# Chunk states of two groups in one two-bank tile, u copied on VectorE, kernel products issued by kind, in a two-layer attention and S5 kernel

## The chip, the cores and the metric

One core of one Trainium2 chip runs the whole network in one launch. The metric is the device time in microseconds (us) of one execution; smaller is better. TensorE is called PE here, VectorE DVE, ScalarE ACT, GpSimd POOL, and SyncE, which only issues DMAs here, SP.

## The reference

Two layers work on 2,048 latent tokens and 256 context tokens of width 1,024. Layer 0 is windowed attention. Layer 1, where the change lies, is a bidirectional diagonal state-space layer (S5): 64 groups of 16 channels, each with 64 complex states and two directions.

```python
for dirn in range(2):
    a_bar = exp(lam * dt)
    b_bar = ((a_bar - 1.0) / lam)[..., None] * b_mat
    bu = einsum('gph,blgh->blgp', b_bar, ug)
    xs = diag_scan(a_bar, bu with the context's last state added at 0)
    y = y + einsum('ghp,blgp->blgh', c_mat, xs).real
out = s5_output(y, z, w_glu, w_out)   # gelu, GLU, silu(z) gate, projection
```

## The kernel before

The state-space layer is done in chunks of 16 tokens: 144 chunks, 16 of them context. It runs in phases, each a Python method. PE does the matmuls of all of them.

**Phase 4** (`phase4`) makes the chunk states `sall`, laid out as 128 partitions x 144 chunks x (re, im) x 64 groups. It goes over 8 slabs of 8 groups. For a slab it needs two tables `er`, `ei` per half slab (4 groups); in even slabs they come by DMA from `ed` (L1416), in odd slabs DVE and POOL build them (L1422 to L1427: two POOL products `em`, four DVE operations). For each group PE transposes the tables into `ep` (four transposes, L1439), ACT copies `ep` to SBUF as `esb` (L1441); PE transposes the group's `u` into `up` (two, L1446), and DVE, or for one group in four (`UPA`, L51) ACT, copies it back over `uy` (L1450, L1448). Then `chunk_states` (L1376) makes four matmuls of 144 columns into the PSUM tile `st` (L1380; the trace has eight records, since a float32 matmul is recorded twice) and ACT writes them to `sall` in three instructions: one direction as it stands (L1382), the other reversed in two pieces (L1383, L1384). Each writes single float32 elements, because neighbouring elements of `sall` in a partition are different groups. `chunk_states` runs one group behind (`LAG4`). `PB` (L50) gives the buffers of `ep`, `up` and `st` in PSUM. Once per slab `up` also carries the context's `u` (L1399, L1400).

The **scan** over chunks on DVE and the **z projection** on PE (`zproj`) follow and run side by side.

**Phase 5** (`phase5`) makes the layer's output in 16 quarters `q` of 4 groups. In steady state `out(q, plan)` goes through the tokens of `P5P` (L36): `S0 S1` state matmuls (L1724) from `xT`, which ACT gathers out of `sall` (L1717, L1719); `K` the kernel products of q+1 (`ker`, L1681 on); `G` tables of q+2 (`gen`); `N` their preparation (`prep`); `O0 O1` own-chunk matmuls (L1735); `B2 B3` both kinds for two more groups; `T` transposes of finished output (L1749). After `O` and `B`, ACT applies Gelu (`ysl`, L1792). `gen` has ACT copy two small parts of the table tile `tab` into `gr` and `gi` (L1582), `prep` has it copy two parts into `cb` (L1671) and four into `g4` (L1676). `ker` accumulates in one PSUM tile `kps`: eight products of 64 columns (L1688), four of 16 columns from `cb` (L1693), each right behind one of the first four, and one with the identity (L1687) ahead of the last. ACT copies `kps` to `ks` (L1697), SP stores `ks` to DRAM as `qqd` (L1699) and loads it back, skewed, as the matrices `mq` (L1708) that `O` and `B` use.

A scheduler sets the order on each engine from the program and its own simulated times; instructions given to `keep` stay in program order. Each engine then runs its list in order.

## Time and profile before

| | us |
|---|---|
| three runs | 2605.39, 2609.28 (median), 2610.87 |
| the profiled execution | 2605.47 |
| its span in the trace | 2603.7 |
| phase 4, first to last transpose or state matmul | about 1527 to 1661 |
| z projection | about 1661 to 1858 |
| phase 5 | about 1859 to 2057 |

The span is the time from the first to the last instruction of the profiled execution; 1.8 us lie around it. "Busy" is the time in which an engine has an instruction running; PE's matmuls overlap, so a busy PE need not be at its peak. A stage is read by its own rows: the share of a whole run says little about which engine holds it up.

### The profile page before, as it was taken

How to read it: one execution, taken by the hardware profiler on the slowest of the kernel's cores; microseconds unless marked ns; L12 is line 12 of the kernel's file. 1: busy time of each engine (PE TensorE's matmuls, PEld its weight loads, DVE VectorE, ACT ScalarE, POOL GpSimd, SP SyncE). 2: the span in 40 equal slices, each digit the busy share in tenths (PEclk: the TensorE clock that was granted, in tenths of full speed). 3: DMA queues.
4: the chain of work that ended last, by engine and by line, in shares of the span. 5: the costliest groups of instructions: out<-in, count | busy, mean ns of one | idle time of the engine just before them, and what ended most of it. 6: DMA issues, size and time to landing. Idle time of an engine off the chain costs nothing. (4 is left out here: it accounts for less than half of the span.)

```text
span 2603.7 us, 43687 instructions
## 1 busy us (share of the span) xinstructions
PE 2493.4 (96%) x15838; PEld 2251.8 (86%) x15838; DVE 1555.8 (60%) x3866; ACT 1151.3 (44%) x2651; POOL 817.2 (31%) x701
## 2 busy tenths in 40 slices
PE   7999999998999999999999999899999899999998
PEld 5999989997988999999899988799877688888887
DVE  4773276636898888888732865698576421012454
ACT  3301210136777777777644349611399610001221
POOL 0321331213545455555432222101265222121221
PEclk9999999998999999999999999999999999999999
DMA  8555456477454434434275552376444322223542
GB/s 282 174 166 169 146 168 195 142 192 196 101 139 106 102 91 104 111 93 104 89 202 176 211 158 83 107 237 236 148 100 103 85 81 81 65 81 122 170 140 79
DMA packets 402312, 360.23 MB, mean 138 GB/s; under 512 B 82921, under 2 KB 345129, under 8 KB 402097
## 3 DMA queue, kind: packets, MB, share of 16 engines
q1 hardware_dynamic: 296216, 286.03, 38.3%
q10 hardware_dynamic: 105880, 71.41, 8.6%
q8 instruction: 126, 2.06, 0.3%
q14 instruction: 90, 0.73, 0.1%
HBM read 250.83 MB, written 106.51 MB: 137 GB/s over the span
## 5 line engine op out<-in xcount | busy, mean ns | idle before, releaser
L117 PE MATMUL mm<-hhl,whi 128*128 128x384 f32 x848 | 285.0, 339 | 1.6 <-DVE whi L109 1.6
L118 PE MATMUL mm<-hhl,whi 128*128 128x384 f32 x848 | 285.3, 337 | 0.7 <-POOL hhl L112 0.7
L119 PE MATMUL mm<-hhl,wlo 128*128 128x384 f32 x848 | 284.8, 336 | 0.7 <-DVE wlo L112 0.7
L950 POOL TENSOR_SCALAR P<-P,ri 128x640 f32<-128x640 f32 (+2 forms) x272 | 209.1, 782 | 232.1 <-DVE ri L948 188.1
L969 DVE TENSOR_TENSOR pl<-pt,ph 128x512 fp32r<-128x512 f32 (+1 forms) x384 | 233.6, 608 | 32.6 <-ACT ph L968 29.5
L928 DVE CUSTOM_DVE_ANT_0 P<-S,mask,sink 128x640 f32<-128x640 f32 (+1 forms) x240 | 209.2, 872 | 60.2 <-PE S L919 55.4
L968 ACT ACTIVATE ph<-pt 128x512 fp32r<-128x512 f32 (+1 forms) x384 | 203.0, 529 | 71.2 <-PE pt L964 68.5
L964 PE MATMUL pt<-ident,P 128*128 128x128 f32 x1312 | 213.2, 275 | 12.5 <-DVE pl L969 4.9
L929 ACT ACTIVATE P<-P,nm 128x640 f32<-128x640 f32 (+1 forms) x256 | 208.4, 814 | 25.3 <-DVE nm L928 8.2
L964 PEld LDWEIGHTS pt<-ident,P 128*128 128x128 f32 x1312 | 157.4, 141 | 30.4 <-POOL P L950 10.5
L117 PEld LDWEIGHTS mm<-hhl,whi 128*128 128x128 f32 x848 | 159.3, 189 | 8.4 <-DVE whi L109 2.9
L112 POOL TENSOR_TENSOR wlo<-wraw,whi 128x512 fp32r<-128x512 f32 x60 | 86.6, 1473 | 248.7 <-DVE whi L109 242.2
L118 PEld LDWEIGHTS mm<-hhl,whi 128*128 128x128 f32 x848 | 159.8, 188 | 3.7 <-issue 2.6
L119 PEld LDWEIGHTS mm<-hhl,wlo 128*128 128x128 f32 x848 | 159.8, 188 | 1.9 <-DVE wlo L112 1.0
L117 PE MATMUL zps<-zh,wzh 128*128 128x256 f32 x512 | 146.5, 287 | 7.1 <-DMA zh<-h1d 4.4
L119 PE MATMUL zps<-zh,wzl 128*128 128x256 f32 x512 | 146.0, 286 | 3.3 <-DVE wzl L112 2.0
L118 PE MATMUL zps<-zh,wzh 128*128 128x256 f32 x512 | 145.4, 285 | 0.0
L1907 DVE TENSOR_TENSOR gy<-gps,gs 128x512 f32<-128x512 f32 x32 | 22.1, 691 | 206.0 <-POOL gs L1905 206.0
L1904 ACT ACTIVATE gs<-gps 128x512 f32<-128x512 f32 x32 | 19.1, 598 | 257.2 <-PE gps L119 257.2
L109 DVE CAST whi<-wraw 128x512 fp32r<-128x512 f32 (+1 forms) x80 | 53.6, 720 | 103.2 <-PE mm L118 96.0
L1905 POOL TENSOR_TENSOR gs<-gs,gz 128x512 f32<-128x512 f32 x32 | 43.8, 1367 | 207.6 <-ACT gs L1904 207.6
L117 PEld LDWEIGHTS zps<-zh,wzh 128*128 128x128 f32 x512 | 99.0, 194 | 9.0 <-DMA zh<-h1d 5.1
(560 smaller groups left out, 7524.5 us busy)
## 6 DMA issues: line engine op xcount, KB each, us to landing
zh<-h1d SPq DMA_DIRECT2D x64, 512.0 KB
qta<-qd SPq DMA_DIRECT2D x144, 128.0 KB
qtb<-qd SPq DMA_DIRECT2D x144, 128.0 KB
wraw<-in_w_ada_dram SPq DMA_DIRECT2D x16, 1024.0 KB
wraw<-in_attn_w_in_dram SPq DMA_DIRECT2D x12, 1024.0 KB
mq<-qqd SPq DMA_DIRECT2D x64, 192.0 KB
qd<-oh ACTq DMA_DIRECT2D x48, 192.0 KB
qd<-ol ACTq DMA_DIRECT2D x48, 192.0 KB
```

The lines of the kernel that those rows point to most:

```text
L109: nc.vector.tensor_copy(hi, src)
L112: (nc.gpsimd if lo_eng == "g" else nc.vector).tensor_tensor(lo, src, hi.bitcast(F32), op=OP.subtract)
L117: nc.tensor.matmul(ps, whi(k), mhi(k), start=first and k == 0, stop=False)
L118: nc.tensor.matmul(ps, whi(k), mlo(k), start=False, stop=False)
L119: nc.tensor.matmul(ps, wlo(k), mhi(k), start=False, stop=last and k == nk - 1)
L928: nc.vector.tensor_tensor_reduce(o, sc, mk, -0.125, nsink[:, h:h + 1], OP.add, OP.min, nm)
L929: nc.scalar.activation(p, p, AF.Exp, bias=nm, scale=-1.0, accum_out=SM[i][:, e:e + 1])
L950: (nc.vector if e >= CTXV else nc.gpsimd).tensor_scalar(P[i][e], P[i][e], ri[:, e:e + 1], 1.0, op0=OP.mult, op1=OP.mult)
L964: ins = nc.tensor.transpose(t[:, c - c0], P[i][e][:, k * 128:(k + 1) * 128], self.ident)
L968: nc.scalar.activation(ph[:, c0:c1], t, AF.Copy)
L969: nc.vector.tensor_tensor(pl[:, c0:c1], t, ph[:, c0:c1].bitcast(F32), op=OP.subtract)
L1905: nc.gpsimd.tensor_tensor(sg, sg, z, op=OP.mult)
```

## The change

In phase 4 `st` becomes a tile of two PSUM banks (128 x 2 x 512, two buffers) that holds the states of two groups, one in each bank. ACT writes a pair of groups with three instructions of twice the elements: of each pair of neighbouring elements in `sall` one comes from the first bank and one from the second. `chunk_states` takes two groups at a time once four are pending. `ep` and `up` go from three buffers to two. All copies of `u` are on DVE.

In phase 5 the first time step of `gr`, `gi` and both halves of `cb` come by SP's DMAs from the table in DRAM, not by ACT from `tab`. `ker` issues its products by kind: four of 64 columns, four of 16, the one with the identity, four of 64.

```diff
-LAG4 = 1
-PB = [3, 3, 2]
-UPA = [1]
+PB = [2, 2, 2]
+UPA = []
@@ phase4
-            def chunk_states(esb, u, g):
-                st = ps.tile([128, 2, 144], F32, name="st", bufs=PB[2])
-                for ri in range(2):
-                    for b in range(2):
-                        nc.tensor.matmul(st[:, ri], esb[:, ri, b], u[:, b * 144:(b + 1) * 144], start=b == 0, stop=b == 1)
+            def chunk_states(pair):
+                g = pair[0][2]
+                st = ps.tile([128, 2, 512], F32, name="st", bufs=PB[2])
+                for i, (esb, u, _) in enumerate(pair):
+                    for ri in range(2):
+                        for b in range(2):
+                            nc.tensor.matmul(st[:, i, ri * 144:(ri + 1) * 144], esb[:, ri, b], u[:, b * 144:(b + 1) * 144],
+                                             start=b == 0, stop=b == 1)
                 sv = sall.rearrange("p j r g -> p r j g")
-                nc.scalar.activation(sv[0:64, :, :, g], st[0:64], AF.Copy)
-                nc.scalar.activation(self.rev(sall, 64, 128, 15, 16, g), st[64:128, :, 0:16], AF.Copy)
-                nc.scalar.activation(self.rev(sall, 64, 128, 143, 128, g), st[64:128, :, 16:144], AF.Copy)
+                tv = st[:, :, 0:288].rearrange("p g (r j) -> p r j g", r=2)
+                nc.scalar.activation(sv[0:64, :, :, g:g + 2], tv[0:64], AF.Copy)
+                nc.scalar.activation(rev2(None, 143, 128, g), tv[64:128, :, 16:144], AF.Copy)
+                nc.scalar.activation(rev2(None, 15, 16, g), tv[64:128, :, 0:16], AF.Copy)
+
+            def rev2(r, j0, n, g):
+                s = sall[64:128]
+                rd = [[64, 2]] if r is None else []
+                return bass.AP(tensor=s.tensor, offset=s.offset + j0 * 128 + g + 64 * (r or 0),
+                               ap=[list(s.ap[0])] + rd + [[-128, n], [1, 2]])
...
-                        if len(pend) > LAG4:
-                            chunk_states(*pend.pop(0))
-            while pend:
-                chunk_states(*pend.pop(0))
+                        if len(pend) == 4:
+                            chunk_states([pend.pop(0), pend.pop(0)])
+            chunk_states(pend)
@@ gen
-            for t, j in ((gr, 4), (gi, 5)):
-                self.keep("E", nc.scalar.activation(t[:, :, 0], tab[:, j], AF.Copy))
+            sl, hf = divmod(q, 2)
+            for t, j in ((gr, 6), (gi, 7)):
+                nc.sync.dma_start(t[:, :, 0], self.tabd[sl, :, j].rearrange("p (g h) -> p g h", g=8)[:, hf * 4:hf * 4 + 4])
@@ prep
-                self.keep("F", nc.scalar.activation(cb[rs], tab[64:128, 4 + ri], AF.Copy))
+                nc.sync.dma_start(cb[rs], self.tabd[q // 2, 64:128, 6 + ri].rearrange("p (g h) -> p g h", g=8)[:, q % 2 * 4:q % 2 * 4 + 4])
@@ ker
             for d in (1, 0):
                 for gg in range(4):
-                    if d == 0 and gg == 3:
-                        nc.tensor.matmul(kp[0:16, :, 1, 0:16], self.ident[0:16, 0:16], kd, start=False, stop=False)
                     ins = nc.tensor.matmul(kp[:, gg, d], bm[:, d, gg].rearrange("p a h -> p (a h)"), g4[:, d, gg],
-                                           start=gg == 0 and d == 1, stop=d == 0 and gg == 3)
+                                           start=gg == 0 and d == 1, stop=gg == 3 and d == 0)
                     if q:
                         self.keep("K", ins)
-                    if d == 1:
-                        nc.tensor.matmul(kp[0:16, gg, 1, 0:16], bm[:, 0, gg, 3], cb[:, gg], start=False, stop=False)
                     yield
+                if d == 0:
+                    break
+                for gg in range(4):
+                    ins = nc.tensor.matmul(kp[0:16, gg, 1, 0:16], bm[:, 0, gg, 3], cb[:, gg], start=False, stop=False)
+                    if q and gg == 0:
+                        self.keep("K", ins)
+                nc.tensor.matmul(kp[0:16, :, 1, 0:16], self.ident[0:16, 0:16], kd, start=False, stop=False)
```

The scheduler's lists move as follows. First, ACT in the middle of phase 4, before (`esb` is a group's copied tables, `sall<-st` its states):

```order
L1441 ACTIVATE esb_18674<-ep 128x512
L1382 ACTIVATE sall<-st 64x2x144
L1383 ACTIVATE sall<-st 64x2x16
L1384 ACTIVATE sall<-st 64x2x128
L1441 ACTIVATE esb_18693<-ep 128x512
L1448 ACTIVATE uy_15780<-up 128x2x128
L1382 ACTIVATE sall<-st 64x2x144
```

and with the change:

```order
L1450 ACTIVATE esb_18703<-ep 128x512
L1450 ACTIVATE esb_18714<-ep 128x512
L1385 ACTIVATE sall<-st 64x2x144x2
L1386 ACTIVATE sall<-st 64x2x128x2
L1387 ACTIVATE sall<-st 64x2x16x2
L1450 ACTIVATE esb_18737<-ep 128x512
```

Two groups' tables are copied one behind the other, then three instructions write both groups' states; no copy of `u` is left on ACT.

DVE at the same stage, where it builds the tables of the slab that comes next, before:

```order
L1423 TENSOR_TENSOR er_18990<-tab_1_18975 128x1024
L1426 TENSOR_TENSOR ei_18991<-tab_1_18975 128x1024
L1400 COPY uy_15775<-up 128x16x16
L1450 COPY uy_15775<-up 128x2x128
L1424 TENSOR_TENSOR er_18990<-er_18990,em_18992 128x1024
L1427 TENSOR_TENSOR ei_18991<-ei_18991,em_18993 128x1024
L1450 COPY uy_15775<-up 128x2x128 x3
```

and with the change:

```order
L1432 TENSOR_TENSOR er_18938<-tab_1_18923 128x1024
L1435 TENSOR_TENSOR ei_18939<-tab_1_18923 128x1024
L1459 COPY uy_15774<-up 128x2x128
L1433 TENSOR_TENSOR er_18938<-er_18938,em_18940 128x1024
L1459 COPY uy_15774<-up 128x2x128
L1436 TENSOR_TENSOR ei_18939<-ei_18939,em_18941 128x1024
L1459 COPY uy_15774<-up 128x2x128
```

The copies are of the slab being worked on (15774), no longer of the next one (15775): `u` is copied less far ahead, and one copy waits behind each one or two table operations.

PE in phase 5, the kernel products of one quarter, before:

```order
L1688 MATMUL kps<-g_23181,bm 64x64
L1693 MATMUL kps<-cb,bm 16x16
L1688 MATMUL kps<-g_23181,bm 64x64 x3
L1687 MATMUL kps<-sall,ident 16x4x16
L1688 MATMUL kps<-g_23181,bm 64x64
L1735 MATMUL yp_23218<-mq,uy_15780 128x256 x2
```

(the first two rows stand there four times in a row), and with the change:

```order
L1695 MATMUL kps<-g_23053,bm 64x64 x4
L1703 MATMUL kps<-cb,bm 16x16 x4
L1706 MATMUL kps<-sall,ident 16x4x16
L1695 MATMUL kps<-g_23053,bm 64x64 x4
L1747 MATMUL yp_23090<-mq,uy_15780 128x256 x2
```

The kind changes three times within a quarter's products, where it changed ten times.

SP in phase 5, before:

```order
L1568 DMA tab_23254<-tabd 128x7x64
L1708 DMA mq<-qqd 128x1x384 x4
L1699 DMA qqd<-ks 128x1x64 x4
L1568 DMA tab_23374<-tabd 128x7x64
L1708 DMA mq<-qqd 128x1x384 x4
```

and with the change:

```order
L1576 DMA tab_23246<-tabd 128x7x64
L1720 DMA mq<-qqd 128x1x384 x4
L1591 DMA gr_23128<-tabd 128x4x16
L1591 DMA gi_23129<-tabd 128x4x16
L1680 DMA cb<-tabd 64x64 x2
L1711 DMA qqd<-ks 128x1x64 x4
```

Four small loads stand between the loads of `mq` and the next stores of `ks`.

## Rows read from the trace of the kernel before

**Rows 1.** Stretches: bounds, length, then busy us (instructions) of PE, PEld, DVE, ACT, POOL; clock, DMA.

```profile
1555.00:1661.00 106.00, 99.29 (x758) 89.85 (x757) 51.64 (x72) 104.01 (x231) 22.66 (x11) 1.00 0.27 79
1680.00:1858.00 178.00, 172.58 (x1427) 170.29 (x1426) 142.06 (x822) 30.08 (x85) 14.39 (x13) 1.00 0.69 229
1880.00:2050.00 170.00, 158.00 (x938) 123.68 (x936) 112.94 (x146) 151.64 (x324) 83.16 (x52) 0.99 0.39 95
```

**Rows 2.** The same view for line 1382 alone, one instruction a group.

```profile
1555.00:1661.00 106.00, 36.48 (x56) 1.00 0.27 79
```

**Rows 3.** Timeline of phase 4, ACT: start us, us, engine, line, operation, tiles.

```profile
1559.08 0.38 ACT L1448 ACTIVATE uy<-up 128x256 f32<-128x256 f32 x1
1559.35 0.66 ACT L1382 ACTIVATE sall<-st 64x288 f32<-64x288 f32 x1
1560.03 0.22 ACT L1383 ACTIVATE sall<-st 64x32 f32<-64x32 f32 x1
1560.12 0.60 ACT L1384 ACTIVATE sall<-st 64x256 f32<-64x256 f32 x1
1560.75 0.60 ACT L1441 ACTIVATE esb<-ep 128x512 f32<-128x512 f32 x1
1561.24 0.65 ACT L1382 ACTIVATE sall<-st 64x288 f32<-64x288 f32 x1
```

**Rows 4.** Timeline of phase 4, PE.

```profile
1561.03 1.15 PE L1380 MATMUL st<-uy,esb 128*128 128x144 f32 x8
1562.01 0.27 PE L1446 MATMUL up<-ident,uy 128*128 128x128 f32 x1
1562.12 0.38 PE L1439 MATMUL ep<-ident,er 128*128 128x128 f32 x2
```

**Rows 5.** Waits in 1555 to 1661: engine, line, waited for: us, times, longest.

```profile
PE st L1380 <- ACT sall L1384: 6.2, 24, 0.6
```

**Rows 6.** Timeline of phase 4, DVE: first and last operation of one half slab's tables.

```profile
1606.23 1.44 DVE L1423 TENSOR_TENSOR er<-tab 128x1024 f32<-128x1024 f32 x1
...
1610.53 2.50 DVE L1427 TENSOR_TENSOR ei<-ei,em 128x1024 f32<-128x1024 f32 x1
```

**Rows 7.** Line 1697, one copy of `ks` a quarter: durations ns, first and last start.

```profile
L1697 ACT ACTIVATE ks<-kps x15: 592/593/597, 1878.1 to 2042.3; 64x512 f32<-64x512 f32 x15
```

**Rows 8.** Waits in phase 5, 1880 to 2050.

```profile
PE yp L1724 <- ACT xT L1719: 11.9, 21, 1.7
```

**Rows 9.** Timeline of phase 5, PE: the kernel products of one quarter.

```profile
1933.55 0.33 PE L1688 MATMUL kps<-g,bm 128*64 128x64 f32 x2
1933.81 0.21 PE L1693 MATMUL kps<-cb,bm 128*16 128x16 f32 x2
1933.95 0.33 PE L1688 MATMUL kps<-g,bm 128*64 128x64 f32 x2
...
1935.16 0.56 PE L1688 MATMUL kps<-g,bm 128*64 128x64 f32 x6
1935.65 0.28 PE L1687 MATMUL kps<-sall,ident 16*16 16x64 f32 x2
1935.86 0.33 PE L1688 MATMUL kps<-g,bm 128*64 128x64 f32 x2
1936.12 1.13 PE L1735 MATMUL yp<-mq,uy 128*128 128x256 f32 x4
```

**Rows 10.** Timeline of phase 5, ACT: the small copies of one quarter.

```profile
1936.85 0.26 ACT L1582 ACTIVATE gr<-tab 128x64 f32<-128x64 f32 x1
1937.01 0.24 ACT L1582 ACTIVATE gi<-tab 128x64 f32<-128x64 f32 x1
1937.28 0.26 ACT L1671 ACTIVATE cb<-tab 64x64 f32<-64x64 f32 x1
1937.55 0.84 ACT L1676 ACTIVATE g<-gr 64x256 f32<-64x256 f32 x2
```

**Rows 11.** Timeline of phase 5, SP: issue times of DMAs.

```profile
1929.00 2.62 SPq L1708 DMA_DIRECT2D mq<-qqd  x4
```

## The prediction

> **What bounds the kernel now.** First the busy times by stretch, because the change touches two stages only. In the z projection between them (second row of [rows 1]) PE is busy for 172.6 of 178 us: whatever the change does earlier or later, that stage keeps its length. In phase 4 (first row) ACT is busy for 104.0 of 106 us and PE for 99.3; in phase 5 (third row) PE for 158.0 and ACT for 151.6 of 170 us. So both touched stages have PE and ACT close together, and the question in each is who waits for whom. PE's clock is at its upper level, 2.4 GHz, in all three (1.00, 1.00, 0.99), so no term below is for the clock.
>
> In phase 4 one state copy stands for one group: 56 in 106 us [rows 2], 1.89 us a group. ACT's timeline shows where they go [rows 3]: from the start of one L1382 to the next, 1561.24 - 1559.35 = 1.89 us, made of 0.68 (L1382 to L1383), 0.09, 0.63 and 0.49 (the table copy) between starts; in one group in four a copy of `u` adds 0.27. PE needs less [rows 4]: the eight records of the state matmuls take 1562.01 - 1561.03 = 0.98 us, a transpose 0.11, and six of those 0.66: 1.64 us a group. And PE does wait for the last state copy, 24 times and 6.2 us [rows 5]. The reader is to see that ACT sets the pace here, by some 0.25 us a group.
>
> In phase 5 a quarter takes (2042.3 - 1878.1) / 14 = 11.73 us [rows 7]. PE waits for the gathered states `xT` in it, 11.9 us in all [rows 8]; PE's idle time in this stretch, 170 - 158 = 12.0 us, is this wait. That is 0.83 us in each of some 14.5 quarters. The rest of a quarter is PE's own work, the kernel products among it.
>
> **Phase 4, ACT.** The state copies of a pair go from six instructions to three, with the same number of elements. The trace has no instruction that writes pairs of neighbouring elements from two banks, so the price is bounded. A copy into single scattered elements costs (0.66 - 0.22) / (288 - 32) = 1.72 ns an element, one between dense tiles (0.60 - 0.38) / (512 - 256) = 0.86 ns [rows 3]. Dear end: a pair's elements cost 1.72 each. Doubling the three instructions adds 0.50, 0.44 and 0.06 us to 0.68 + 0.63 + 0.09, in all 2.40 us, and two table copies 0.98: 3.38 us a pair, 1.69 a group, and 56 x (1.89 - 1.69) = 11 us gained. Cheap end: 0.86 each, 0.54 + 0.49 + 0.09 + 0.98 = 2.10 us a pair; then PE is the bound. In these 106 us it has about 55 groups of state matmuls (54 us) and 51 of tables (22 us) to do and about 53 of `u` (12 us), 88 to 89 us, so 17 us are gained. I take the dear end, since the reading side is scattered even if the writing side is half as much so. That ACT then stands at 1.69 and PE at 1.64 leaves no slack for either.
>
> The rows show that scattered single elements cost twice what dense ones do. The Trainium skill (SBUF — State Buffer, Specifications) says that SBUF has 16-byte lines and needs at least two hits on a line for full bandwidth; by that, pairs would be written at the dense price, and the sum would be 5 us better. The Trainium skill (PSUM — Partial Sum Buffer, Specifications) gives PSUM 8-byte lines and warns that non-contiguous patterns slow matmuls markedly; it says nothing of ACT, but if it held there, reading the two banks in turn would be slow. No row here shows either.
>
> **Phase 4, the copies of `u`.** 16 of 0.27 us leave ACT (12 of them in this stretch, 3 us; the 1.89 us above contain 0.06 of them a group, which the 1.69 leaves out). DVE gains 16 of about 0.4 us, 6 us, and is busy for 51.6 of 106: on average it hides them. In bursts it may not. Building the tables of half a slab took from 1606.23 to 1613.03, 6.8 us with two copies within [rows 6]; with four it is 7.5 us, and four groups at 1.69 take 6.8. Six such halves lie behind the start of the phase. At worst each is late by 0.7 us and PE's transposes wait: 4 us; at best the build starts early enough: nothing. I take 2. The phase's start, before 1555, is set by loads and the first tables and stays. At the end PE's first z matmuls need loads into tiles that the last state matmuls free, as now; one copy of a pair is longer than one of a group, and I take 0 to 2 us, 0.5. Phase 4 gains 11 - 2 - 0.5 = **about 9 us**, with ends of 3 (dear copies and all the losses, somewhat uneven) and 16.
>
> **Phase 5, PE.** A quarter's products take 1936.12 - 1933.55 = 2.57 us [rows 9]: four times 0.40 for a 64-column one and the 16-column one behind it (0.26 and 0.14), then three of 0.16 behind their own kind, 0.21 for the identity, 0.26 for the last. A product thus takes 0.10 more when another kind follows. By kind: eight times 0.16, two changes of 0.10, 0.21 for the identity, and four 16-column ones. These take at most 0.14 each, the value beside the other kind, and at least 0.04, a quarter of a 64-column one. That is 1.28 + 0.20 + 0.21 + 0.16 to 0.56 = 1.85 to 2.25 us: 0.3 to 0.7 gained, and I take 0.4. The products lie on PE's own path, so 14 quarters gain 4 to 10 us, 6 taken.
>
> **Phase 5, ACT.** Four small copies leave it: between starts 0.16, 0.27 and 0.27 for `gr`, `gi` and the first `cb` [rows 10], and the second `cb` like the first, together 0.97 us a quarter. They stand between `ks` and the Gelu copies, ahead of the `xT` that PE waits for. PE's waits are 0.83 us a quarter, so at most that is gained, 12 us; but part of ACT's lead is lost again, since the Gelu copy of `B2` needs PE's result. At the other end, if that copy sets the time, nothing is gained. I take half, 0.4 us in 14.5 quarters: 6 us. Phase 5 gains **12 us**, with ends of 4 and 22.
>
> **SP and DMA.** Each quarter SP issues four more loads. Their price is not in the trace; a load of `mq` takes 2.62 / 4 = 0.65 us to issue [rows 11], so they take up to 2.6 us, on a queue that now holds four stores, four `mq` loads and one table in 11.73 us. I take them as hidden: SP has some 6 us free in a quarter, and `gr` and `gi` are wanted by the copies behind the next `ks`, five microseconds after the `mq` loads ahead of them are out (1931.62 against 1936.85 [rows 10, 11]). If this cover is gone, `mq` comes late.
>
> **Sum.** 9 + 12 = 21 us off the profiled execution's 2605.5: 2584.5. That execution is 3.8 us below the median of the three runs, 2609.3, from which the same gain leads to 2588. I take **2586 us**.
>
> **The rivals.**
>
> *Reading two banks in turn is slow* (slower). If each element costs the scattered price once for reading and once for writing, 3.44 ns, a pair's three instructions take 2.17 + 1.95 + 0.26, and with the table copies 5.36 us, where two groups take 3.78 now: 28 pairs lose 44 us, phase 5 gives 12 back, and the time is 2605.5 + 32 = **2637**. The point from which phase 4 loses: a pair's copies at 2.80 us, 2.1 ns an element. For it speaks that no row shows such a read; against it, that every scattered copy here costs the same 1.7 ns, as if one slow side hid the other. Chance 0.08. What the Trainium skill says of PSUM's lines, above, would be its reason.
>
> *The small loads hold up SP* (no change, or little gained). The loads of `cb` have one buffer and wait for the kernel products of the quarter before; the stores of `ks` are queued right behind them, then the `mq` loads, then PE's own-chunk matmuls. If this chain were PE's bound, the 2.6 us of issue would come in full: 14 x 2.6 = 36 us lost against 21, 2620; if only the pair of `cb` loads (1.3 us) gets into it, 18 are lost: **2602**. Against it: `mq` is issued at 1929.00 to 1931.62 and its first use is not waited for anywhere in the rows of waits; the `cb` loads can go out while ACT still copies `ks`. Chance 0.10.
>
> *DVE or the `B2` path takes ACT's place.* The wait that goes in phase 4 comes back as transposes that wait for tables, in phase 5 as Gelu copies that wait for PE: phase 4 gains 3, phase 5 only its 4 on PE: 2605.5 - 7 = **2598**. DVE's burst of 7.5 us against 6.8 speaks for it, its low average against. Chance 0.12.
>
> *Pairs are written at the dense price and both engines gain in full.* 15 + 20 = 35 us: **2570**. For it: PE's need of 1.64 us and its 0.83 us of idle time are real. Chance 0.15.
>
> **How the numbers follow.** The forecast has 0.55, with its own range of 2576 to 2596. The difference that a measurement of this kernel can tell from none is 0.2%, 5 us, so the border lies at 2604. Faster: the forecast, the dense case, nearly all of the third rival and half of the second, 0.55 + 0.15 + 0.10 + 0.05 = 0.85. Slower: the first and a little of the second, 0.08. No change: the rest, 0.07. The range from 2569 to 2602 reaches to the dense case and to the third rival, and leaves out the first and part of the second.
>
> **What would show it.** Right: the new state copies (576 and 512 elements) at about 1.1 us each or less, their pace below 3.5 us a pair, ACT no longer waited for by the state matmuls; phase 4 over by about 1652; a quarter of phase 5 at 10.7 to 11.1 us, the products at 2.0 to 2.3. Wrong: state copies above 1.3 us; PE's transposes waiting for tables or `u` by more than 5 us; waits of `yp` for `mq`, or of `ks` or `g4` copies for DMAs; PE's clock at its lower level, 1.2 GHz, in phase 4, where it stands at 1.00 now.

## The result, and the profile after

The changed kernel takes 2591.9 us (median of four runs, 2589.7 to 2594.2) where the kernel before takes 2610.1 (2605.4 to 2611.0): a ratio of 0.9934, with a 95% interval of 0.9917 to 0.9951. By the medians 18.2 us are gained. The profiled execution took 2593.2 us with a span of 2591.0; against the profiled execution before, whose span is 2603.7, that is 12.7 us. The two figures differ because the execution before that was profiled is 4.6 us below its kernel's median and the one after 1.3 us above. The predicted time was 2586, its range 2569 to 2602.

The changed file's lines are up to 12 higher: the state matmuls are L1381, the state copies L1385, L1386 and L1387, the table copies L1450, the copies of `u` L1459 (of the context's `u` L1409), DVE's table operations L1432 to L1436, the kernel products L1695, L1703 and L1706, `ks` L1709, `gr` and `gi` by DMA L1591.

First the two touched stages, by the windows that answer to [rows 1] (bounds, length, then busy us and instructions of PE, PEld, DVE, ACT, POOL; clock, DMA):

```profile
1555.00:1656.00 101.00, 91.24 (x762) 88.67 (x761) 67.11 (x90) 67.97 (x134) 21.61 (x12) 1.00 0.29 83
1872.50:2030.30 157.80, 142.32 (x910) 113.79 (x911) 126.13 (x149) 134.66 (x261) 83.44 (x52) 0.98 0.48 108
```

In phase 4 ACT was busy for 98% of its window and is now for 67%. It is not the bound any more. But PE is not busy all the time either: 91.2 of 101 us, where it should be if it set the pace. From the first transpose of `u` to the last state matmul, start to start, the phase takes 127.5 us (1528.5 to 1656.0) where it took 132.6. The z projection keeps its length, as the prediction had it: 203.8 us from its first matmul to phase 5's first, 203.6 before.

The three state copies of the changed kernel, 32 of each, from the lines' own views (durations in ns, least/median/most, first and last start), to be held against [rows 3]:

```profile
L1385 ACT ACTIVATE sall<-st x32: 663/672/696, 1539.8 to 1656.3; 64x576 f32<-64x576 f32 x32
L1386 ACT ACTIVATE sall<-st x32: 602/612/624, 1540.5 to 1657.0; 64x512 f32<-64x512 f32 x32
L1387 ACT ACTIVATE sall<-st x32: 198/205/215, 1541.0 to 1657.5; 64x64 f32<-64x64 f32 x32
```

The first two copy 576 and 512 elements in the time in which one group's 288 and 256 were copied (0.66 and 0.60 us). Between 64 and 576 elements this is (672 - 205) / 512 = 0.91 ns an element, near the cheap price of 0.86.

What PE waits for in phase 4 (1527 to 1661) of the changed kernel, the answer to [rows 5] (us in all, times, longest):

```profile
PE up L1408 <- DVE uy L1459: 5.8, 3, 1.9
PE up L1455 <- DVE uy L1459: 4.4, 6, 1.2
PE ep L1448 <- DMA ei<-ed: 3.1, 1, 3.1
...
PE up L1455 <- DVE uy L1409: 1.5, 2, 1.2
PE ep L1448 <- DVE ei L1436: 1.0, 2, 0.5
```

No state matmul waits for ACT any more. In its place stand 12.7 us of waits for DVE, nearly all of them transposes of `u` that need a buffer of `up` which DVE has not copied out. Before, the same window has 6.2 us for ACT and 4.6 for DVE, so by PE's matmul rows it waits no less than it did, although the phase is 5.1 us shorter. Part of the waiting before stands in these rows as busy time: for as many matmuls (911 and 912 records) PE counts as busy for 120.3 us of the phase before and for 111.7 now. The rows of its weight loads (PEld), busy for 109.1 and 107.7 us, show the trade better. Their waits in the same window, before:

```profile
PEld st L1380 <- ACT sall L1384: 16.0, 40, 0.9
PEld up L1446 <- DVE uy L1450: 2.2, 1, 2.2
```

and now:

```profile
PEld up L1408 <- DVE uy L1459: 6.5, 3, 2.2
PEld up L1455 <- DVE uy L1459: 5.6, 6, 1.4
...
PEld up L1455 <- DVE uy L1409: 2.0, 2, 1.4
```

With the smaller entries, 16.0 us for ACT's state copies and 5.5 for DVE have become 15.6 for DVE.

One such place in the timelines, first DVE, then POOL, then PE's next transpose (start, us, engine, line; in brackets the idle time before and what ended it):

```profile
1602.18 1.22 DVE L1433 TENSOR_TENSOR er<-er,em 128x1024 f32<-128x1024 f32 x1
1603.31 0.42 DVE L1459 COPY uy<-up 128x256 f32<-128x256 f32 x1
1603.64 2.83 DVE L1436 TENSOR_TENSOR ei<-ei,em 128x1024 f32<-128x1024 f32 x1
1606.40 0.41 DVE L1459 COPY uy<-up 128x256 f32<-128x256 f32 x1
1606.73 2.83 DVE L1432 TENSOR_TENSOR er<-tab 128x1024 f32<-128x1024 f32 x1
...
1603.47 1.93 POOL L1431 TENSOR_TENSOR em<-tab 128x1024 f32<-128x1024 f32 x1 [16.75 <-DVE er L1433]
1606.56 1.93 POOL L1434 TENSOR_TENSOR em<-tab 128x1024 f32<-128x1024 f32 x1 [1.16 <-DVE ei L1436]
...
1606.87 0.44 PE L1455 MATMUL up<-ident,uy 128*128 128x128 f32 x2 [0.57 <-DVE uy L1459]
...
1611.09 0.44 PE L1408 MATMUL up<-ident,ucs 128*128 128x128 f32 x2 [1.93 <-DVE uy L1459]
```

A DVE operation on these tables takes 1.22 us or 2.83. It takes 2.83 where a POOL product began just before it, and ends 1.07 us after that product's end (1603.47 + 1.93 = 1605.40; 1603.64 + 2.83 = 1606.47). The copy of `u` queued behind it comes late, and PE stands.

In phase 5 the copy of `ks`, from its line's own view as in [rows 7]:

```profile
L1709 ACT ACTIVATE ks<-kps x15: 591/591/593, 1872.5 to 2030.3; 64x512 f32<-64x512 f32 x15
```

and one quarter's products on PE's timeline, as in [rows 9]:

```profile
1926.93 0.68 PE L1695 MATMUL kps<-g,bm 128*64 128x64 f32 x8
1927.54 0.36 PE L1703 MATMUL kps<-cb,bm 128*16 128x16 f32 x8
1927.84 0.28 PE L1706 MATMUL kps<-sall,ident 16*16 16x64 f32 x2
1928.05 0.68 PE L1695 MATMUL kps<-g,bm 128*64 128x64 f32 x8
1928.66 0.48 PE L1747 MATMUL yp<-mq,uy 128*128 128x256 f32 x1
```

A quarter takes (2030.3 - 1872.5) / 14 = 11.27 us, 0.46 less than before. Its products take 1928.66 - 1926.93 = 1.73 us where they took 2.57. So the products alone gave more than the quarter gained, and something was given back. The waits between the first and the last `ks`, PE's (to be held against [rows 8]) and ACT's, show what:

```profile
PE yp L1736 <- ACT xT L1731: 12.4, 14, 1.6
...
ACT g L1685 <- DMA gr<-tabd: 8.2, 5, 2.1
...
ACT g L1685 <- DVE bm L1628: 4.1, 2, 2.4
```

and so does the place of one of these waits on the timelines of SP and ACT:

```profile
1923.39 2.60 SPq L1720 DMA_DIRECT2D mq<-qqd  x4
1926.03 0.46 SPq L1591 DMA_DIRECT2D gr<-tabd  x1
1926.53 0.51 SPq L1591 DMA_DIRECT2D gi<-tabd  x1
...
1928.76 0.59 ACT L1709 ACTIVATE ks<-kps 64x512 f32<-64x512 f32 x1 [0.24 <-PE kps L1695]
1931.41 0.84 ACT L1685 ACTIVATE g<-gr 64x256 f32<-64x256 f32 x2 [2.06 <-DMA gr<-tabd]
```

ACT, rid of 0.97 us of small copies a quarter, now waits for the load that took their place. That load was issued at 1926.03, behind the four of `mq`, and ACT got on at 1931.41, 5.4 us later. The other wait of the same copies, 4.1 us for DVE's `bm`, is not there in the kernel before. PE's wait for `xT` did not fall.

### The profile page after: what moved, and what is told of

It reads as the page before. It is cut to its first block, busy times and chain, and to the rows that moved or that the text cites. A ratio compares the mean times of both kernels' runs of the same rounds, so it can differ in the third digit from the quotient of the medians.

```text
span 2591.0 us, 43577 instructions
## 1 busy us (share of the span) xinstructions
PE 2470.1 (95%) x15838; PEld 2239.4 (86%) x15838; DVE 1580.9 (61%) x3882; ACT 1095.0 (42%) x2479; POOL 810.9 (31%) x701
## 6 DMA issues: line engine op xcount, KB each, us to landing
qta<-qd SPq DMA_DIRECT2D x144, 128.0 KB
qtb<-qd SPq DMA_DIRECT2D x144, 128.0 KB
```

## The experiments

Each was timed against the kernel before on the same chip. Two lengths from the profile of each stand beside its time: phase 4 from the first transpose of `u` to the last state matmul, and phase 5 from the first to the last copy of `ks`. Kernels with the same code in the stage differ by up to 3 us in the first (132.6, 132.4, 133.9 with the code before; 127.5, 128.0, 126.4 with that of the change; 117.4, 115.7, 118.7 in e5, e8 and e11) and by up to 4 us in the second (157.5 to 161.8 with that of the change). The kernel before was timed anew beside each set of kernels, with medians from 2607.5 to 2610.1 us; the first of them stands in the table. So kernels of two sets are compared by their ratios.

| kernel | median us | ratio to before (95%) | phase 4 | phase 5 |
|---|---|---|---|---|
| before | 2610.1 | 1 | 132.6 | 164.2 |
| the change | 2591.9 | 0.9934 (0.9917 to 0.9951) | 127.5 | 157.8 |
| e1_phase4 | 2602.8 | 0.9972 (0.9961 to 0.9982) | 128.0 | 164.0 |
| e2_korder | 2599.4 | 0.9966 (0.9954 to 0.9978) | 132.4 | 158.5 |
| e3_loads | 2606.1 | 0.9990 (0.9976 to 1.0003) | 133.9 | 162.9 |
| e4_u_act | 2592.2 | 0.9933 (0.9921 to 0.9945) | 127.9 | 157.6 |
| e5_em_dve | 2581.1 | 0.9903 (0.9890 to 0.9917) | 117.4 | 157.5 |
| e6_gr_dve | 2587.6 | 0.9920 (0.9906 to 0.9933) | 126.4 | 151.1 |
| e7_apart | 2591.5 | 0.9937 (0.9925 to 0.9950) | 124.4 | 161.8 |
| e8_both | 2575.5 | 0.9875 (0.9860 to 0.9890) | 115.7 | 150.9 |
| e9_far | 2593.9 | 0.9951 (0.9939 to 0.9964) | 130.2 | 159.6 |
| e10_before_em | 2602.0 | 0.9980 (0.9971 to 0.9988) | 130.8 | 164.3 |
| e11_xpair | 2583.5 | 0.9910 (0.9898 to 0.9922) | 118.7 | 159.3 |
| e12_both_u | 2571.4 | 0.9853 (0.9840 to 0.9867) | 113.4 | 151.2 |

### The three parts alone

e1_phase4 is the kernel before with the hunks of phase 4 and nothing else:

```diff
-PB = [3, 3, 2]
-UPA = [1]
+PB = [2, 2, 2]
+UPA = []
...
-                st = ps.tile([128, 2, 144], F32, name="st", bufs=PB[2])
+                st = ps.tile([128, 2, 512], F32, name="st", bufs=PB[2])
...
-                            chunk_states(*pend.pop(0))
+                            chunk_states([pend.pop(0), pend.pop(0)])
```

> Only the edits in phase 4 (pair tiles, u copied on DVE, buffers 2/2/2); phase 5 as before. Theory A: the two stages add up as the changed kernel's trace shows them. There phase 5 begins at 1859.8 us where it began at 1864.1, so this kernel gains 4 us (ratio to before 0.998), the copies of 576 elements take 0.67 us, and PE still waits for DVE's copies of u by more than 10 us. Rival B: phase 4 gains the 9 us of the prediction and the single trace understates it (ratio 0.9965, first z matmul by 1652).

Theory A is near: phase 4 is 4.6 us shorter, and PE waits for DVE's `u` copies there too (5.8, 5.1 and 0.9 us). By the time it is 7 us, between the two theories, and the interval (4.7 to 10.2 us) takes in the 9 us of B and the ratio of A, 0.998.

e2_korder is the kernel before with the hunk of `ker` alone:

```diff
             for d in (1, 0):
                 for gg in range(4):
-                    if d == 0 and gg == 3:
-                        nc.tensor.matmul(kp[0:16, :, 1, 0:16], self.ident[0:16, 0:16], kd, start=False, stop=False)
                     ins = nc.tensor.matmul(kp[:, gg, d], ...)
...
-                    if d == 1:
-                        nc.tensor.matmul(kp[0:16, gg, 1, 0:16], bm[:, 0, gg, 3], cb[:, gg], start=False, stop=False)
                     yield
+                if d == 0:
+                    break
+                for gg in range(4):
+                    ins = nc.tensor.matmul(kp[0:16, gg, 1, 0:16], bm[:, 0, gg, 3], cb[:, gg], start=False, stop=False)
...
+                nc.tensor.matmul(kp[0:16, :, 1, 0:16], self.ident[0:16, 0:16], kd, start=False, stop=False)
```

> Only the order of the kernel products, by kind; everything else as before, so ACT still makes the four small copies. Theory A: the products are on PE's path and give nearly all of phase 5's gain: they take 1.7 us a quarter where they took 2.57, and 6 to 11 us are gained (ratio 0.996 to 0.9977). Rival B: ACT holds the pace of phase 5 as long as it has the small copies, and PE's time saved turns into waits for xT: at most 3 us gained (ratio above 0.9988), PE's waits for xT up by 8 us or more.

Theory A: 8.9 us, with phase 5 shorter by 5.7. In that stretch PE is busy for 144.4 us where it was for 152.8, so the order takes 8.4 us of work off PE, and 2.7 come back as idle time.

e3_loads is the kernel before with the hunks of `gen` and `prep`: the first time steps of `gr` and `gi`, and `cb`, by DMA:

```diff
-            for t, j in ((gr, 4), (gi, 5)):
-                self.keep("E", nc.scalar.activation(t[:, :, 0], tab[:, j], AF.Copy))
...
+            for t, j in ((gr, 6), (gi, 7)):
+                nc.sync.dma_start(t[:, :, 0], self.tabd[sl, :, j]...)
...
-                self.keep("F", nc.scalar.activation(cb[rs], tab[64:128, 4 + ri], AF.Copy))
+                nc.sync.dma_start(cb[rs], self.tabd[q // 2, 64:128, 6 + ri]...)
```

> Only the loads: first time step of gr, gi and cb by DMA; order of the products and phase 4 as before. Theory A: ACT gets rid of 0.97 us a quarter but waits for gr's load instead (8 us in the changed kernel's phase 5), so between 2 us gained and 2 us lost (ratio 0.9992 to 1.0008). Rival B: ACT's relief is worth the 6 us that the prediction gave it (ratio 0.9977), with PE's waits for xT falling from 11 us to about 5.

Mostly A: 2.6 us, within the noise of none. Its views of the waits show both halves of the trade (ACT and PE in phase 5):

```profile
PE yp L1725 <- ACT xT L1720: 8.1, 13, 1.4
...
ACT g L1677 <- DMA gr<-tabd: 8.9, 7, 3.5
```

PE's waits for `xT` do fall, by 3 us, but ACT spends 8.9 us waiting for the loads out of some 12 that the copies had cost. The three parts together give 0.9972, 0.9966 and 0.9990, or 19 us, and the whole change 17: within the intervals they add up.

### Phase 4: who holds it now

e4_u_act gives half of the `u` copies back to ACT, which has time to spare:

```diff
-UPA = []
+UPA = [1, 3]
```

> The changed kernel, but the copies of u of two groups in four go back to ACT, which is idle for some 30% of phase 4 there. Theory A: PE now waits for DVE, where the copies of u stand behind the table operations; half of them off DVE take away at least half of the 16 us that PE idles there, so phase 4 ends 5 to 9 us earlier than in the changed kernel and the ratio to before is about 0.991. Rival B: ACT in its fixed order becomes the pace again, or the tables and not the copies are what is late: no gain over the changed kernel (ratio 0.993 or more).

Rival B, by its second half: no gain, though ACT had the room. PE's transposes wait for DVE's remaining `u` copies for 8.8 us in all; these still stand behind table operations of up to 2.84 us. So the number of copies is not what makes them late.

e5_em_dve makes the products `em` on DVE:

```diff
-                    nc.gpsimd.tensor_tensor(m, pw(1), bb(1), op=OP.mult)
+                    nc.vector.tensor_tensor(m, pw(1), bb(1), op=OP.mult)
...
-                    nc.gpsimd.tensor_tensor(m2, pw(1), bb(0), op=OP.mult)
+                    nc.vector.tensor_tensor(m2, pw(1), bb(0), op=OP.mult)
```

> The changed kernel, but the 16 products em of phase 4 are made by DVE, not POOL. Theory A: in the changed kernel's trace a DVE table operation takes 2.83 us where a POOL product of 1.93 us runs beside it and 1.22 us where none does, and the copies of u wait behind; with POOL out of it every table operation takes 1.2 us, PE's waits for DVE in phase 4 fall from 12.7 us to 6 or less, and phase 4 ends 3 to 7 us earlier (ratio to before 0.991 to 0.992). Rival B: 16 more operations of 1.2 us, 19 us in all, make DVE the bound: the copies of u come as late as now or later (ratio 0.9935 or above).

Theory A, and beyond its upper end: phase 4 takes 117.4 us, 10.1 less than in the changed kernel, and the time falls by 10.8 us by the medians, by 8 by the ratios. One line of DVE's table operations, from the line's own view in the changed kernel:

```profile
L1436 DVE TENSOR_TENSOR ei<-ei,em x8: 1209/2833/2840, 1545.2 to 1643.0; 128x1024 f32<-128x1024 f32 x8
```

in this kernel:

```profile
L1436 DVE TENSOR_TENSOR ei<-ei,em x8: 1209/1214/1216, 1545.4 to 1633.8; 128x1024 f32<-128x1024 f32 x8
```

and what PE still waits for DVE in phase 4 of this kernel:

```profile
PE up L1408 <- DVE uy L1459: 2.6, 3, 0.9
...
PE up L1455 <- DVE uy L1459: 0.5, 2, 0.2
PE up L1455 <- DVE uy L1409: 0.3, 1, 0.3
```

DVE has 16 operations more, and PE waits for it 3.4 us instead of 12.7: no table operation takes longer than 1.23 us now.

e10_before_em makes the same edit in the kernel before.

> The kernel before, with nothing changed but the 16 products em of phase 4, made by DVE and not POOL. Theory A: before the change ACT holds phase 4 at 1.89 us a group and DVE's stretched operations are hidden behind it, so this gives 0 to 3 us (ratio 0.999 to 1.000), where the same edit gave 10.8 us on the changed kernel: ACT's relief by the pairs is then worth some 15 us, of which DVE held back 10. Rival B: DVE's stretched operations cost PE the same 10 us before the change too (ratio 0.996).

Neither exactly: 5 us (3 to 8) by the times, 1.8 us by the length of phase 4. In its trace the table operations are at 1.21 us, and PE waits for ACT's last state copy for 6.2 us in 20 waits, much as in [rows 5]. So ACT held the phase, and the edit is worth much less there than on the changed kernel. By the stage lengths the pairs alone give 4.6 us, `em` on DVE alone 1.8, and both 15.2, which is more than the two and the 3 us of spread together. By the times it is 7, 5 and, taking phase 5's two parts off e5's 25, about 14; their errors are too wide to show the difference. Where the other 3 us of this kernel come from stays open.

### What sets the price of the state copies

e7_apart pairs groups two apart (0 and 2, 1 and 3):

```diff
-                nc.scalar.activation(sv[0:64, :, :, g:g + 2], tv[0:64], AF.Copy)
+                nc.scalar.activation(sv[0:64, :, :, g:g + 3:2], tv[0:64], AF.Copy)
...
-                               ap=[list(s.ap[0])] + rd + [[-128, n], [1, 2]])
+                               ap=[list(s.ap[0])] + rd + [[-128, n], [2, 2]])
...
-                            chunk_states([pend.pop(0), pend.pop(0)])
+                            chunk_states([pend.pop(0), pend.pop(g % 4 // 2)])
```

> The changed kernel, but a pair is made of groups two apart (0 and 2, 1 and 3, and so on), so that the two elements read in turn from the two banks no longer land beside each other in sall. Theory A: the price of the state copies is that of the writes: an element that stands alone costs 1.72 ns, one with its neighbour half of it. Then the 576 elements take 1.16 us and the 512 take 1.05 where they take 0.67 and 0.61, a pair needs 3.5 us on ACT, and phase 4 is as long as before the change or longer, 132 to 137 us from its first u transpose to its last state matmul (ratio 0.996 to 0.999). Rival B: it is the number of elements to an instruction that sets the price, or the reads: the copies stay at 0.67 us, phase 4 at 127.5 and the ratio at 0.993.

Rival B as far as neighbours go: the copies stay at 0.67 and 0.61 us. But the experiment was too weak for what it asked, as both elements still lie within the same four columns of `sall`, 16 bytes. So the next puts them 128 bytes apart:

```diff
-                nc.scalar.activation(sv[0:64, :, :, g:g + 2], tv[0:64], AF.Copy)
+                nc.scalar.activation(sv[0:64, :, :, g // 2:g // 2 + 33:32], tv[0:64], AF.Copy)
...
-                return bass.AP(tensor=s.tensor, offset=s.offset + j0 * 128 + g + 64 * (r or 0),
-                               ap=[list(s.ap[0])] + rd + [[-128, n], [1, 2]])
+                return bass.AP(tensor=s.tensor, offset=s.offset + j0 * 128 + g // 2 + 64 * (r or 0),
+                               ap=[list(s.ap[0])] + rd + [[-128, n], [32, 2]])
```

> The changed kernel, but the state of group 2k is written to column k of sall and that of group 2k+1 to column k+32, so that the two elements of a pair land 128 bytes apart; sall then holds every group in another column than the scan and phase 5 take it from. In the run with pairs two apart the copies kept their price, but there the two elements still lay 8 bytes from each other. Theory A: what counts is that two writes in turn fall close to each other; 128 bytes apart they cost the 1.72 ns of single elements, the 576 elements take about 1.16 us, the 512 about 1.05, and phase 4 has 132 to 137 us (ratio 0.996 to 0.999). The Trainium skill (SBUF: State Buffer, Specifications) would have it so: lines of 16 bytes with at least two hits each. Rival B: what counts is not the distance of the writes; the copies stay at 0.67 and 0.61 us (ratio 0.993).

Theory A for the price. The same two lines as above, of this kernel:

```profile
L1385 ACT ACTIVATE sall<-st x32: 1157/1182/1216, 1538.3 to 1657.2; 64x576 f32<-64x576 f32 x32
L1386 ACT ACTIVATE sall<-st x32: 1042/1066/1107, 1539.5 to 1658.5; 64x512 f32<-64x512 f32 x32
```

Reads, element counts and instructions are the same; only the distance of the writes differs, and the price goes from 0.67 to 1.18 us. It did not cost the time that A gave it, though: phase 4 takes 130.2 us, 2.7 more than in the changed kernel and within the spread, for 32 pairs that each need 1.1 us more on ACT. DVE holds the phase either way: PE waits for its copies of `u` for 10.9 us here (11.7 in the changed kernel), and no state matmul waits for ACT.

### Phase 5: what the loads cost

e6_gr_dve has DVE copy the first time step of `gr` and `gi` from the table tile; `cb` is still loaded.

```diff
             for t, j in ((gr, 6), (gi, 7)):
-                nc.sync.dma_start(t[:, :, 0], self.tabd[sl, :, j]...)
+                nc.vector.tensor_copy(t[:, :, 0], tab[:, j - 2])
```

> The changed kernel, but the first time step of gr and gi is copied by DVE from the table tile, not loaded by DMA; cb is still loaded. Theory A: the 8.2 us that ACT waits for gr's load in phase 5 are gone, ACT comes to xT earlier, and 3 to 6 us of PE's waits for xT go (ratio 0.991 to 0.9925; first to last ks 152 to 155 us where the changed kernel has 157.8). Rival B: PE's waits for xT have their cause elsewhere, in the Gelu copies ahead of xT that wait for PE itself: within 1.5 us of the changed kernel (ratio 0.9930 to 0.9938).

Theory A, by the stage: phase 5 takes 151.1 us, 6.7 less and outside the spread. By the medians 4.3 us are gained, by the ratios 4, with intervals that overlap. PE's and ACT's waits in it, first to last `ks`:

```profile
PE yp L1736 <- ACT xT L1731: 4.5, 7, 0.9
PE yp L1747 <- DMA mq<-qqd: 1.2, 2, 1.0
...
ACT ysl L1804 <- PE yp L1736: 8.1, 8, 1.8
```

PE waits for `xT` for 4.5 us where it waited for 12.4, and now ACT's Gelu copies wait for PE. So ACT's relief was worth about what the prediction gave it; the wait for the load had eaten it. The 4.1 us for which ACT waited for DVE's `bm` are gone here as well; how they hang together with the load was not tried apart.

### Versions that beat both kernels

e8_both joins the two edits by DVE, e5's and e6's:

```diff
-                    nc.gpsimd.tensor_tensor(m, pw(1), bb(1), op=OP.mult)
+                    nc.vector.tensor_tensor(m, pw(1), bb(1), op=OP.mult)
...
-                nc.sync.dma_start(t[:, :, 0], self.tabd[sl, :, j]...)
+                nc.vector.tensor_copy(t[:, :, 0], tab[:, j - 2])
```

> The changed kernel with both edits, em by DVE in phase 4 and the first time step of gr and gi by DVE in phase 5. The two stages lie apart, so the gains over the changed kernel should add: by theory A of each 6 to 13 us (ratio 0.9885 to 0.991), by the rivals none (0.9934).

The gains add, and come out a little above theory A's upper end: 2575.5 us, 16.4 below the changed kernel by the medians (10.8 and 4.3 for the two alone) and 15 by the ratios (8 and 4).

e11_xpair tries the pairs on the reading side, too: ACT gathers `xT` for two groups at once.

```diff
-            xt = pools[1].tile([128, 2, 128], F32, name="xT", bufs=2)
-            ins = nc.scalar.activation(xt[0:64], sall[0:64, 15:143, :, g].rearrange("p j r -> p r j"), AF.Copy)
+            if gg % 2:
+                return xpair.pop()
...
+            xt = pools[2].tile([128, 2, 2, 128], F32, name="xT", bufs=2)
+            xv = xt.rearrange("p g r j -> p r j g")
+            ins = nc.scalar.activation(xv[0:64], sall[0:64, 15:143, :, g:g + 2].rearrange("p j r g -> p r j g"), AF.Copy)
...
+            xpair.append(xt[:, 1])
+            return xt[:, 0]
```

> The run with both edits by DVE, and ACT also gathers xT for two groups in one pair of instructions of 512 elements, reading neighbouring elements of sall and writing each to its group's half of a tile. Theory A: pairs are as cheap to read as to write, about 0.65 us for 512 elements where 256 take 0.65 now; ACT is rid of some 2.5 us a quarter, PE's last waits for xT (4.5 us) go, and 2 to 5 us are gained over that run (ratio 0.9855 to 0.987). Rival B: scattered reads cost the same for each element whether in pairs or not, 1.3 us for 512, and since the first group of a pair now waits for both, PE waits longer: ratio 0.988 or more.

Rival B by the time: 8 us slower than e8_both (ratio 0.9910 against 0.9875). The gather of 512 elements takes 1.12 us where two of 256 take 1.30 together, so the price is nearer to B's. But the loss is not the one that B names: PE does not wait for `xT` at all any more. Between the first and the last `ks` it waits instead

```profile
PE ytp L1769 <- ACT uy L1773: 9.3, 7, 1.4
PE kps L1695 <- DVE bm L1628: 6.2, 1, 6.2
```

for ACT's copies of the transposed output and, once, for DVE. Why these come later was not tried. In this gather the reads come in pairs, but the writes alternate between two places 1 KB apart; which side sets the price was not tried apart.

e12_both_u is e8_both with half of the `u` copies on ACT:

```diff
-UPA = []
+UPA = [1, 3]
```

> The run with both edits by DVE, with the copies of u of two groups in four on ACT. Theory A: phase 4 is now PE's own (busy 110 of 116 us there), and what is left of its waits for DVE's copies of u is 5 us, so this gives 0 to 3 us (ratio 0.9863 to 0.9877). Rival B: more copies of u ahead of the state copies hold ACT's order up, and phase 4 is 3 us longer (ratio 0.9887).

Theory A, a little beyond: 2571.4 us, the lowest median of all, ratio 0.9853, 20 us below the changed kernel. Phase 4 takes 113.4 us, and its window shows PE itself as the bound (columns as in the first windows):

```profile
1533.40:1647.00 113.60, 109.39 (x913) 107.81 (x912) 71.99 (x93) 88.31 (x189) 0.00 (x0) 0.98 0.41 114
```

The edit that gave nothing in e4 gives 4 us over e8_both here, where the copies of `u` no longer stand behind stretched operations. This gain is not clear of noise: the two intervals overlap, and the 2.3 us by the stage are within its spread.

## Why the prediction was right, and where its steps failed

The time lies in the range, in the direction forecast, 5.9 us above the figure. In part that is luck. Against the profiled execution the sum was 21 us and 12.7 came: phase 4 gave 5 instead of 9, and phase 5, from its first matmul to its last `ks`, 7.7 instead of 12. The terms beneath were off by more, and their errors cancel: the state copies and the kernel products were cheaper than forecast, and the copies of `u` and SP's loads gave that back.

**The price of the state copies (phase 4): wrong end taken.** "I take the dear end, since the reading side is scattered even if the writing side is half as much so." The copies take 0.67 and 0.61 us, not 1.16 and 1.04. Reading two banks in turn costs nothing that shows, and e9 shows that the price hangs on where the writes fall: side by side or 8 bytes apart 0.67 us (the change, e7), 128 bytes apart 1.18 (e9). The Trainium skill (SBUF — State Buffer, Specifications) speaks of 16-byte lines that want two hits each, and by it the prediction's own text had the sum 5 us better (its two ends, 11 and 17 us, lie 6 apart). The three runs agree with it, but no distance between 8 and 128 bytes was tried, so that the line has 16 bytes is not shown here. The first rival, a slow two-bank read, is out. By the prediction's own sum this term alone would have given phase 4 the 17 us of the cheap end.

**The copies of `u` on DVE (phase 4): mis-sized.** The prediction took 2 us, with 4 as the worst, from a half slab's burst of 7.5 us against 6.8. The burst is near that (7.8 us a half: two of them from 1599.57 to 1615.25), but the sum of a burst is not what PE waits for. With two buffers of `up` each copy of `u` is due within about a group's time, 1.64 us, and a single operation ahead of it takes 2.83. That loss is the 12.7 us of waits. Taking POOL's products away leaves 3.4 of them and makes the phase 10.1 us shorter (e5); moving half of the copies leaves its length as it was (e4). This is the third rival's mechanism in phase 4, "transposes that wait", and its figure of 3 us there is nearer to the 5 measured than the forecast's 9. The row that should have told is in [rows 6]: its first and last operations work on equally many elements and take 1.44 and 2.50 us, and the prediction read over the difference.

**The kernel products (phase 5): right mechanism, too small.** 0.3 to 0.7 us a quarter was given, 0.4 taken; the quarter shown saves 0.84. In the stretch between first and last `ks` PE is busy 10.5 us less, 0.75 a quarter. Two parts of the sum were too dear. The four 16-column products take 0.30 us in all, inside the bounds, where the 0.4 taken leaves 0.48 for them; and the two changes of kind put at 0.10 each don't show: the eight large ones take 1.22 and the identity 0.21, which with 0.30 is all of the 1.73.

**ACT's small copies (phase 5): right size, but not received.** Of the 6 us taken, e3 shows 1 to 3. e6 shows 4 to 7 more once DVE makes the copies of `gr` and `gi`.

**The SP loads: wrongly costed at nothing.** "`gr` and `gi` are wanted by the copies behind the next `ks`, five microseconds after the `mq` loads ahead of them are out." That reckoned with the issue time alone, and with a cover that the change itself makes shorter: at the place shown the loads of `mq` are out at 1926.0 and `ks` is done at 1929.35, 3.3 us later, while the load of `gr` is in use 5.4 us after its issue. Such a load is late about every third quarter, by 8.2 us in all. It is not the second rival's chain: PE does not wait for `mq` in the changed kernel.

Two of the signs that the prediction named for being wrong are there: "PE's transposes waiting for tables or `u` by more than 5 us" (12.7) and waits "of `ks` or `g4` copies for DMAs" (8.2).

The z projection and PE's clock behaved as said: 203.8 us against 203.6, and 1.00 in phase 4's window. The quarter, 11.27 us, is just above the 10.7 to 11.1 that was to show the forecast right; phase 4 was to be over by 1652 and was at 1656.

## What to carry to other kernels

When one engine is relieved, look in the queue of the engine that comes next for the longest single operation and for how soon the small one behind it is due: an average hides this, and the sign here was an operation that shows two durations in the profile. A copy replaced by a load costs the time from issue to use, here 5.4 us behind four larger loads on the same queue, so compare that with when it is wanted. And when scattered results are written, try to write two that are close together in turn: here reading them from two PSUM banks cost nothing that shows.

## What the runs showed of the hardware

A DVE operation with two inputs from SBUF takes 1.22 us alone and 2.83 beside a POOL product of 1.93 us that started first; with POOL idle (e5) all of them take 1.21 to 1.23. DVE's copies out of PSUM keep their 0.41 us beside the same product (L1409 and L1459 at 1584.64 and 1584.97, with a POOL product from 1584.80 to 1586.73):

```profile
1581.89 2.83 DVE L1436 TENSOR_TENSOR ei<-ei,em 128x1024 f32<-128x1024 f32 x1
1584.64 0.41 DVE L1409 COPY uy<-up 128x256 f32<-128x256 f32 x1
1584.97 0.41 DVE L1459 COPY uy<-up 128x256 f32<-128x256 f32 x1
...
1584.80 1.93 POOL L1434 TENSOR_TENSOR em<-tab 128x1024 f32<-128x1024 f32 x1 [1.16 <-DVE ei L1436]
```

The Trainium skill (SBUF — State Buffer, Who interferes with whom) says that a VectorE instruction with two SBUF inputs and a GpSimd instruction that reads SBUF exclude each other, and that the later one waits until the first is done. The rows agree: 2.83 us is the 1.76 that the product had left plus 1.07. By that rule POOL's products, each starting together with an operation of DVE's, were themselves the cost, and the prediction did not use it. The operations of 1.44 and 2.50 us in [rows 6] follow it too. POOL's products beside them, in the kernel before:

```profile
1604.66 1.93 POOL L1425 TENSOR_TENSOR em<-tab 128x1024 f32<-128x1024 f32 x1 [1.16 <-DVE ei L1427]
1610.03 1.93 POOL L1422 TENSOR_TENSOR em<-tab 128x1024 f32<-128x1024 f32 x1 [3.43 <-DVE er L1424]
```

They end at 1606.59 and 1611.96, and the two operations at 1607.67 and 1613.03, again 1.08 and 1.07 us later, however long the overlap was.

ACT writes 576 float32 results in 0.67 us when each two written in turn lie at most 8 bytes apart, and in 1.18 us when they lie 128 bytes apart, from the same two PSUM banks.
